# GpSimd scales the softmax probabilities by a scalar per partition instead of a repeated column

## Chip, core and metric

The kernel runs on one core of one Trainium2 chip. The metric is the device time of one execution in microseconds (us). A core has five engines that the text names as the profile does: PE (TensorE, matmuls), PEld (its weight loads), DVE (VectorE), ACT (ScalarE), POOL (GpSimd) and SP (SyncE, which issues most transfers).

## What is computed

A decoder trunk of two layers on 512 tokens plus 16 learned meta tokens in front, width 1024. Each layer has one input projection and two token mixers: a multi-scale causal pooling, and a latent attention with 8 heads. The change lies in the attention's softmax:

```python
s = jnp.einsum('bqhd,bkhd->bhqk', q[:, q0:kend], k[:, :kend]).astype(jnp.float32) * scale
s = jnp.where(valid, s, MASK_VALUE)
p = jax.nn.softmax(s, axis=-1).astype(v.dtype)
outs.append(jnp.einsum('bhqk,bkhd->bqhd', p, v[:, :kend]))
```

Everything around it is matrix products with the layer's weights:

```python
proj = h @ w_in[l]
y_pool = (pool_mix(u_pool, pool_w_group[l], pool_scale[l]) * jax.nn.silu(z_pool)) @ pool_w_up[l]
y_mla = (o_mla * jax.nn.silu(z_mla)) @ mla_w_up[l]
merged = jax.nn.sigmoid(g_pool) * y_pool + jax.nn.sigmoid(g_mla) * y_mla
h_res = h_res + merged @ w_out[l]
```

## The kernel before

Activations stand with channels on the 128 partitions and the 528 tokens along the free axis. Nearly every product is made in three matmuls (`mm3`, lines 188, 191 and 192): weight and activation are each split into a high and a low part, and high x high, high x low and low x high are summed. A weight chunk of 128x512 is fetched by SP (`raw`), its high part is made by ACT (line 183, `whi`) and its low part by DVE (line 184, `wlo`, which reads `raw` and `whi`). `stream()` goes through all these products in a fixed plan and loads three chunks ahead.

The heads of attention are woven into this stream: `go` calls `prep`, `head` and `pv` head by head, and `gap` fills the time between them with stream work. `prep` makes a head's keys: DVE scales one half (line 847) and POOL the other (line 848). `head` makes the scores of four blocks of 128 queries in PSUM, masks them and takes the row extreme on DVE (line 877), makes the exponentials with their row sums on ACT (line 884) and the reciprocals of the sums, `rs`, on DVE (line 917). The exponentials of the four blocks stand in `pt`: block 0 and 1 in one tile `pa` (144 and 272 columns), block 2 in `pb` (400) and block 3 in `pc` (528), the last two in slots that the profile calls `cq`. The 128 queries of a block are its partitions, so `rs[:, i:i+1]` is one number per partition. POOL then scales each block by it: the 16 columns of the meta tokens go into `pm` (line 922, two heads side by side), the rest is scaled in place (line 924). That makes eight POOL instructions per head, one after the other, for 16 heads.

`pv` reads the result for the head before: PE transposes the scaled tiles (line 944), ACT and DVE split them (`split`, lines 295 and 296), and PE multiplies them with the values (lines 949 and 950). In every second head ACT and DVE also split `pm` (lines 937 to 939) for a small product of its own (line 955). ACT's line 964 and DVE's line 965 empty the one PSUM bank `o`. In the second layer, `mixed`, `fast` and `got_gp` add combinations of activations on DVE between the heads, for a product of the gates that needs seven block products instead of eight.

Instructions are written out in Python order, but the order on each engine is set by a scheduler when the kernel is built (`schedule_with_timeline_sim=True`), which places instructions by the durations that it assumes for them. Each engine then runs its own list in that order and waits on semaphores.

Of the kernel before, what the change touches and what calls it, by code (L numbers as in the profile page):

```python
# [14 lines left out]
ALU = mybir.AluOpType  # L15
# [3 lines left out]
P = 128  # L19
# [3 lines left out]
NM = 16  # L23
# [49 lines left out]
def trunk(ctx, tc, xT, pos, win, wkr, wqb, wkb, wvb, wgr, wpu, wmu, wout, gains, const, yT):  # L73
    nc = tc.nc
    pe, act, dve, gp, sp = nc.tensor, nc.scalar, nc.vector, nc.gpsimd, nc.sync
# [11 lines left out]
    def nm(s):  # L87
        uid[0] += 1
        return f"{s}_{uid[0]}"

    def slot(tag, dt=F32, bufs=1, w=W):
        return sl.tile([P, w], dt, tag=tag, name=nm(tag), bufs=bufs)
# [10 lines left out]
    def sct():  # L103
        return pp.tile([P, 512], F32, tag="S", name=nm("S"), bufs=3)
# [82 lines left out]
    def mm3(out, wh, wl, xh, xl, start, stop, more=False, hold=False):  # L187
        first = pe.matmul(out, wh, xh, start=start, stop=False, skip_group_check=more)  # L188
        if hold:
            behind(first, newest[0])  # L190
        pe.matmul(out, wh, xl, start=False, stop=False, skip_group_check=more)  # L191
        newest[0] = pe.matmul(out, wl, xh, start=False, stop=stop, skip_group_check=more)  # L192
        past.append((clk[0], newest[0]))
# [163 lines left out]
    class Layer:  # L357
# [503 lines left out]
        def head(self, h, kq, prev, between):  # L861
            kh, kl, qh, ql = kq
            odd = h % 2
            nqs, hold = self.nqs, h == 0
            pa = slot("pa", bufs=2, w=416)
            pb = slot(f"cq{8 + odd}")
            pc = slot(f"cq{10 + odd}")
            bia = sm.tile([P, 5], F32, tag="bia", name=nm("bia"), bufs=2)
            rs = sm.tile([P, 5], F32, tag="rs", name=nm("rs"), bufs=2)

            def scores(i, out, a, b):
                q0 = NM + P * i
                mm3(out, qh[:, q0:q0 + P], ql[:, q0:q0 + P], kh[:, a:b], kl[:, a:b], True, True,
                    hold=hold and i == 1)

            def top(i, c, sv, mask):
                dve.tensor_tensor_reduce(out=sv, in0=sv, in1=mask, scale=nqs[:, i, h:h + 1], scalar=3e38,  # L877
                                         op0=ALU.add, op1=ALU.min, accum_out=bia[:, c:c + 1])

            def causal(n):  # L880
                return maskw[:, 512 - n:]

            def expo(i, c, sv, pv):
                act.activation(pv, sv, AF.Exp, scale=-1.0, bias=bia[:, i:i + 1], accum_out=rs[:, c:c + 1])

            pt = [pa[:, 0:144], pa[:, 144:416], pb[:, 0:400], pc[:, 0:T]]
            sa = sct()
            s1, s3 = sa[:, 0:272], sa[:, 272:272 + SPL]
            scores(1, s1, 0, 272)
            scores(3, s3, 0, SPL)  # L890
            top(1, 1, s1, causal(272))
            top(3, 4, s3, maskw[:, 0:SPL])
            sb = sct()
            s2 = sb[:, 0:400]
            scores(2, s2, 0, 400)
            if not self.last:
                mm3(sb[0:NM, 400:416], qh[:, 0:NM], ql[:, 0:NM], kh[:, 0:NM], kl[:, 0:NM], True, True)
                dve.tensor_add(self.smeta[:, h, :], sb[0:NM, 400:416], cst[0:NM, C_MM:C_MM + NM])
            top(2, 2, s2, causal(400))
            expo(1, 1, s1, pt[1])  # L900
            expo(2, 2, s2, pt[2])
            self.gap()
            between()
            self.pv(prev, (0, 1))
            self.gap()
            sc = sct()
            s0, s4 = sc[:, 0:144], sc[:, 144:144 + T - SPL]
            scores(3, s4, SPL, T)
            scores(0, s0, 0, 144)
            top(3, 3, s4, causal(T - SPL))  # L910
            top(0, 0, s0, causal(144))
            dve.tensor_tensor(out=bia[:, 3:4], in0=bia[:, 3:4], in1=bia[:, 4:5], op=ALU.min)
            expo(3, 4, s3, pt[3][:, 0:SPL])
            expo(3, 3, s4, pt[3][:, SPL:T])
            expo(0, 0, s0, pt[0])
            dve.tensor_add(rs[:, 3:4], rs[:, 3:4], rs[:, 4:5])
            dve.reciprocal(rs[:, 0:4], rs[:, 0:4])  # L917
            if odd == 0:
                self.pm = sm.tile([P, 4, 32], F32, tag="pm", name=nm("pm"), bufs=2)
            for i in range(4):  # L920
                n = pt[i].shape[1]
                gp.tensor_mul(self.pm[:, i, 16 * odd:16 * odd + 16], pt[i][:, 0:NM],  # L922
                              rs[:, i:i + 1].to_broadcast([P, NM]))
                gp.tensor_mul(pt[i][:, NM:], pt[i][:, NM:], rs[:, i:i + 1].to_broadcast([P, n - NM]))  # L924
            return h, pt, self.pm

        def pv(self, prev, js):
# [365 lines left out]
```

## Time and profile before

| | |
|---|---|
| three runs | 788.27, 788.89 and 788.9 us; median 788.89 |
| the profiled execution | 788.28 us, of which the span of the program's instructions is 786.4 us |
| PE, PEld | busy 778.8 and 713.4 us |
| DVE, ACT | busy 558.8 and 427.1 us |
| POOL | busy 210.9 us in 275 instructions |
| PE's granted clock | full speed throughout |
| DMA | 97.6 MB, 124 GB/s on average |

The times in the profile are those of the profiled execution. An engine counts as busy from the start to the end of each of its instructions; PE's ends are modelled. The heads of the first layer lie between about 190 and 335 us of the span, those of the second between about 580 and 720 us.

### The profile page before, as it was taken

Reading aid. Unit: us, or ns where it says so; the run is one execution under the profiler, and the core shown is the slowest. Engines: PE = TensorE matmul, PEld = TensorE weight load, DVE = VectorE, ACT = ScalarE, POOL = GpSimd, SP = SyncE. Lnnn points to the kernel's source line nnn. Section 1 sums busy time; section 2 is a strip of 40 time slices with the busy share of each in tenths; the row PEclk is TensorE's granted clock in tenths of the full one; section 3 lists DMA queues with packets and bytes.
Section 4 is the critical chain, followed back from the end, with each engine's and each line's share of the span. In section 5 each row is a group of like instructions: output and inputs, shape, how many; then the busy total and the mean of one; then the engine's idle time right before and its main releaser. Section 6 shows DMA issues by size and latency. Waiting matters only on the chain.

```text
span 786.4 us, 15094 instructions
## 1 busy us (share of the span) xinstructions
PE 778.8 (99%) x5445; PEld 713.4 (91%) x5445; DVE 558.8 (71%) x1229; ACT 427.1 (54%) x974; POOL 210.9 (27%) x275
## 2 busy tenths in 40 slices
PE   9999999999999999999999999999999999999998
PEld 8999899999999999999997898887778999887887
DVE  5848778447788977685355487775897899874932
ACT  8545655635656665643354455556657676654421
POOL 1034504002434342153000145122004323440600
PEclk9999999999999999999999999999999999999999
DMA  6242343434645435647742422435233454462372
GB/s 243 82 101 84 99 120 102 128 106 117 136 122 126 116 90 112 167 103 176 206 141 81 109 81 79 138 97 167 95 111 112 118 153 126 121 202 68 99 231 100
DMA packets 60907, 97.61 MB, mean 124 GB/s; under 512 B 9744, under 2 KB 18320, under 8 KB 60832
## 3 DMA queue, kind: packets, MB, share of 16 engines
q1 hardware_dynamic: 57520, 90.61, 38.8%
q0 software_dynamic: 2304, 4.20, 4.3%
q10 hardware_dynamic: 1008, 1.84, 0.7%
q8 instruction: 43, 0.70, 0.4%
q14 instruction: 32, 0.26, 0.1%
HBM read 88.64 MB, written 14.23 MB: 131 GB/s over the span
## 4 chain that ended last, share of the span: by engine, by line
PE 91%; DVE 4%; DMA 2%; issue 1%; ACT 1%; ACTq 0%; DVEq 0%
PE mm L188 27%; PE mm L192 27%; PE mm L191 26%; PE mm L944 2%; PE S L191 2%; PE S L192 2%; PE S L188 1%; DVE wlo L184 1%; PE o L950 1%; PE o L949 1%; PE S L498 1%; PE mm L400 1%; DMA xb<-xT 1%; DMA raw<-win 1%; DVE hl L296 0%
## 5 line engine op out<-in xcount | busy, mean ns | idle before, releaser
L188 PE MATMUL mm<-hh,whi 128*128 128x264 f32 (+2 forms) x1080 | 333.9, 311 | 0.1
L191 PE MATMUL mm<-hl,whi 128*128 128x264 f32 (+2 forms) x1080 | 332.5, 309 | 0.4 <-DVE hl L296 0.4
L192 PE MATMUL mm<-hh,wlo 128*128 128x264 f32 (+2 forms) x1080 | 332.1, 310 | 0.4 <-DVE wlo L184 0.4
L184 DVE TENSOR_TENSOR wlo<-raw,whi 128x512 fp32r<-128x512 f32 (+2 forms) x263 | 197.7, 756 | 108.8 <-ACT whi L183 105.3
L183 ACT ACTIVATE whi<-raw 128x512 fp32r<-128x512 f32 (+2 forms) x263 | 157.8, 603 | 179.3 <-PE mm L191 114.6
L188 PEld LDWEIGHTS mm<-hh,whi 128*128 128x128 f32 x1080 | 202.9, 188 | 11.8 <-ACT racc L958 0.5
L191 PEld LDWEIGHTS mm<-hl,whi 128*128 128x128 f32 x1080 | 203.3, 188 | 11.1 <-DVE hl L296 0.9
L192 PEld LDWEIGHTS mm<-hh,wlo 128*128 128x128 f32 x1080 | 202.5, 188 | 10.5 <-DVE wlo L184 1.1
L700 POOL TENSOR_TENSOR racc<-racc,tmp 128x264 f32<-128x264 f32 (+1 forms) x15 | 14.2, 950 | 144.2 <-ACT tmp L699 119.8
L192 PE MATMUL mm<-cq,wlo 128*128 128x264 f32 (+2 forms) x140 | 43.5, 313 | 0.6 <-DVE wlo L184 0.6
L188 PE MATMUL mm<-cq,whi 128*128 128x264 f32 (+2 forms) x140 | 44.0, 314 | 0.0
L191 PE MATMUL mm<-cq,whi 128*128 128x264 f32 (+2 forms) x140 | 43.4, 311 | 0.0
L848 POOL TENSOR_TENSOR tmp<-kp,bc 64x528 f32<-64x528 f32 x16 | 23.7, 1484 | 68.5 <-PE mm L815 44.4
L1049 POOL TENSOR_TENSOR tmp<-tmp,xb 128x264 f32<-128x264 f32 (+1 forms) x24 | 27.2, 1155 | 50.4 <-DVE tmp L1047 38.9
L877 DVE CUSTOM_DVE_ANT_0 S<-S,maskw,nqs 128x288 f32<-128x288 f32 (+4 forms) x80 | 38.3, 497 | 3.0 <-PE S L192 2.8
L922 POOL TENSOR_TENSOR pm<-pa,rs 128x16 f32<-128x16 f32 x32 | 10.9, 340 | 96.7 <-DVE rs L917 88.6
L188 PE MATMUL mm<-u,whi 128*128 128x264 f32 (+1 forms) x108 | 35.2, 326 | 0.1
L296 DVE TENSOR_TENSOR tl<-mm,th 128x512 fp32r<-128x512 f32 (+1 forms) x64 | 29.4, 481 | 7.7 <-ACT th L295 6.5
L192 PE MATMUL mm<-u,wlo 128*128 128x264 f32 (+1 forms) x108 | 34.7, 322 | 0.0
L924 POOL TENSOR_TENSOR cq<-cq,rs 128x384 f32<-128x384 f32 (+1 forms) x32 | 32.8, 1024 | 0.0
L191 PE MATMUL mm<-kn,whi 128*128 128x264 f32 (+1 forms) x96 | 30.6, 320 | 0.0
L188 PE MATMUL mm<-q,whi 128*128 128x264 f32 (+1 forms) x96 | 29.9, 323 | 0.6 <-ACT q L295 0.4
(309 smaller groups left out, 1472.3 us busy)
## 6 DMA issues: line engine op xcount, KB each, us to landing
raw<-win SPq DMA_DIRECT2D x139, 256.0 KB, 2.7
raw<-wout SPq DMA_DIRECT2D x32, 256.0 KB, 3.3
bc<-kdr SPq DMA_DIRECT2D x16, 264.0 KB, 4.1
raw<-wpu SPq DMA_DIRECT2D x16, 256.0 KB, 2.8
wsum<-win SPq DMA_DIRECT2D x16, 256.0 KB, 3.3
raw<-wmu SPq DMA_DIRECT2D x16, 256.0 KB, 2.8
raw<-wsum SPq DMA_DIRECT2D x16, 256.0 KB, 3.2
raw<-wqb SPq DMA_DIRECT2D x12, 256.0 KB, 2.6
```

The lines of the kernel that those rows point to most:

```text
L183: act.activation(hi[:, :n], raw[:, :n], AF.Copy)
L184: dve.tensor_sub(lo[:, :n], raw[:, :n], hi[:, :n].bitcast(F32))
L188: first = pe.matmul(out, wh, xh, start=start, stop=False, skip_group_check=more)
L191: pe.matmul(out, wh, xl, start=False, stop=False, skip_group_check=more)
L192: newest[0] = pe.matmul(out, wl, xh, start=False, stop=stop, skip_group_check=more)
L296: dve.tensor_sub(lo[:, a:b], src, hi[:, a:b].bitcast(F32))
L700: self.acc_last = gp.tensor_add(self.acc[:, a:b], self.acc[:, a:b], t[:, :b - a])
L848: gp.tensor_mul(kf[r0:r0 + 64, :], self.kp[r0:r0 + 64, :], bc[r0:r0 + 64, :])
L877: dve.tensor_tensor_reduce(out=sv, in0=sv, in1=mask, scale=nqs[:, i, h:h + 1], scalar=3e38, op0=ALU.add, op1=ALU.min, accum_out=bia[:, c:c ...
L924: gp.tensor_mul(pt[i][:, NM:], pt[i][:, NM:], rs[:, i:i + 1].to_broadcast([P, n - NM]))
L944: pe.transpose(tr[:, P * (i - j):P * (i - j + 1)], pt[i][:, NM + P * j:NM + P * (j + 1)], ident)
L1049: gp.tensor_add(t[:, :b - a], t[:, :b - a], self.am[m][:, a:b])
```

## The change

Where POOL multiplied a tile by `rs`'s column read again for every element (a second tensor with a step of zero), it now runs the operation that multiplies a tile by one scalar per partition, read from the same place. The values, the tiles and the number of instructions are the same, in both layers.

```diff
             for i in range(4):
-                n = pt[i].shape[1]
-                gp.tensor_mul(self.pm[:, i, 16 * odd:16 * odd + 16], pt[i][:, 0:NM],
-                              rs[:, i:i + 1].to_broadcast([P, NM]))
-                gp.tensor_mul(pt[i][:, NM:], pt[i][:, NM:], rs[:, i:i + 1].to_broadcast([P, n - NM]))
+                gp.tensor_scalar(self.pm[:, i, 16 * odd:16 * odd + 16], pt[i][:, 0:NM], rs[:, i:i + 1], None, op0=ALU.mult)
+                gp.tensor_scalar(pt[i][:, NM:], pt[i][:, NM:], rs[:, i:i + 1], None, op0=ALU.mult)
```

The changed kernel is two lines shorter, so line 944 of before is line 942 of after, and 937 is 935. The scheduler assumes another duration for the new operation, and so the order on PE, DVE, ACT and SP changes too, within the heads of both layers; outside them it is the same.

On PE, in the first head of the first layer, the transposes of the scaled tiles stood together. `pa` holds blocks 0 and 1, `cq_459` block 2 and `cq_460` block 3; `mm_2825` and `mm_2836` are the PSUM banks that they are transposed into. Before and after:

```order
L191 MATMUL mm_2750<-hl_21_143,whi_2746 128x264
L192 MATMUL mm_2750<-hh_20_142,wlo_2747 128x264
L944 MATMUL mm_2825<-cst,pa_2530 128x128 x2
L944 MATMUL mm_2825<-cst,cq_459_2531 128x128
L944 MATMUL mm_2825<-cst,cq_460_2532 128x128
L944 MATMUL mm_2836<-cst,pa_2530 128x128
L944 MATMUL mm_2836<-cst,cq_459_2531 128x128
L944 MATMUL mm_2836<-cst,cq_460_2532 128x128
```

```order
L191 MATMUL mm_2750<-hl_21_143,whi_2746 128x264
L192 MATMUL mm_2750<-hh_20_142,wlo_2747 128x264
L942 MATMUL mm_2825<-cst,pa_2530 128x128 x2
L942 MATMUL mm_2836<-cst,pa_2530 128x128
L188 MATMUL mm_2751<-hh_14_136,whi_2746 128x264
L191 MATMUL mm_2751<-hl_15_137,whi_2746 128x264
L192 MATMUL mm_2751<-hh_14_136,wlo_2747 128x264
L942 MATMUL mm_2825<-cst,cq_459_2531 128x128
L942 MATMUL mm_2836<-cst,cq_459_2531 128x128
```

The transposes of block 2 moved behind three matmuls; those of block 3 come further down, out of this piece.

On PE, in the fourth head of the second layer, `cq_1584_8244` is block 3 and `cq_1583_8243` block 2; `S_8620` are scores of the next head. Before:

```order
L188 MATMUL S_8620<-kh_8425,qhl_105 128x144
L191 MATMUL S_8620<-kl_8426,qhl_105 128x144
L192 MATMUL S_8620<-kh_8425,qhl_106 128x144
L944 MATMUL mm_8549<-cst,cq_1584_8244 128x128
L944 MATMUL mm_8560<-cst,pa_8242 128x128
L944 MATMUL mm_8560<-cst,cq_1583_8243 128x128
L944 MATMUL mm_8560<-cst,cq_1584_8244 128x128
L188 MATMUL mm_8468<-hh_14_136,whi_8579 128x256
```

After, the transposes of block 3 stand here:

```order
L192 MATMUL mm_8530<-sq_7748,wlo_8602 128x256
L188 MATMUL mm_8530<-rinv_7752,whi_8601 128x256
L191 MATMUL mm_8530<-rinv_7752,whi_8601 128x256
L192 MATMUL mm_8530<-rinv_7752,wlo_8602 128x256
L942 MATMUL mm_8549<-cst,cq_1584_8244 128x128
L942 MATMUL mm_8560<-cst,cq_1584_8244 128x128
L953 MATMUL mm_8570<-identr,pmr_8545 96x128 x4
```

They moved from right behind the scores to behind the 12 matmuls into `mm_8468` and the 12 into `mm_8530`.

On ACT, at the same head, the split of `pm` (line 937, now 935). Before:

```order
L183 ACTIVATE whi_8526<-raw_8524 128x512
L623 ACTIVATE sv_8481<-mm_8468 128x256
L937 ACTIVATE pmr_8545<-pm_8119 128x4x32
L964 ACTIVATE tmp_8450<-o_8313 64x512
L884 ACTIVATE cq_1636_8484,rs_8487<-S_8497,bia_8486 128x400
L183 ACTIVATE whi_8579<-raw_8577 128x512
```

After:

```order
L183 ACTIVATE whi_8526<-raw_8524 128x512
L623 ACTIVATE sv_8481<-mm_8468 128x256
L884 ACTIVATE pa_8483,rs_8487<-S_8488,bia_8486 128x272
L183 ACTIVATE whi_8579<-raw_8577 128x512
L962 ACTIVATE tmp_8450<-o_8313 64x512
L183 ACTIVATE whi_8601<-raw_8599 128x512
L935 ACTIVATE pmr_8545<-pm_8119 128x4x32
```

Two weight splits, an exponential and the emptying of `o` now stand ahead of it. On POOL the eight instructions of a head stand as before, with TENSOR_SCALAR in place of TENSOR_TENSOR; one L848 of the first layer moved ahead of a head's eight.

## The prediction

> **What bounds the kernel now.** I read the page's busy line first, then the chain that ended last, then busy time by stretch, and only then GpSimd (POOL).
>
> ```profile
> PE 778.8 (99%) x5445; PEld 713.4 (91%) x5445; DVE 558.8 (71%) x1229; ACT 427.1 (54%) x974; POOL 210.9 (27%) x275
> PE 91%; DVE 4%; DMA 2%; issue 1%; ACT 1%; ACTq 0%; DVEq 0%
> ```
>
> Busy time by stretch: start and end, length, then PE, weight loads, DVE, ACT and POOL, clock, DMA share and GB/s.
>
> ```profile
> 190.00:335.00 145.00, 144.65 (x1175) 142.82 (x1174) 115.41 (x285) 86.95 (x224) 52.63 (x80) 1.00 0.53 124
> 580.00:700.00 120.00, 119.10 (x779) 107.90 (x779) 109.05 (x263) 83.87 (x216) 45.69 (x70) 1.00 0.45 135
> ```
>
> TensorE (PE) is busy 99% of the span and carries 91% of the chain; POOL stands nowhere on it. The two stretches are the attention heads of the two layers, where the edited lines run. PE idles 0.35 us in the first and 0.90 us in the second. So little can be won: whatever POOL saves, PE's work stays. What can be lost depends on who waits for POOL. DVE is the second engine to watch: in the second layer's heads it is busy 109.05 of 120 us, 91%, with 10.95 us idle; in the first layer's it has 29.6 us.
>
> **The change, part by part.** It swaps 128 POOL instructions one for one, eight in each of 16 heads: four that copy 16 scaled columns into pm and four that scale the rest in place. Groups by line and shape (busy us, mean ns):
>
> ```profile
> L924 POOL TENSOR_TENSOR cq<-cq,rs 128x512 f32<-128x512 f32 x16 | 17.2, 1078 | 0.0
> L924 POOL TENSOR_TENSOR cq<-cq,rs 128x384 f32<-128x384 f32 x16 | 15.5, 970 | 0.0
> L924 POOL TENSOR_TENSOR pa<-pa,rs 128x256 f32<-128x256 f32 x16 | 11.4, 711 | 0.0
> L924 POOL TENSOR_TENSOR pa<-pa,rs 128x128 f32<-128x128 f32 x16 | 7.5, 471 | 0.0
> L922 POOL TENSOR_TENSOR pm<-cq,rs 128x16 f32<-128x16 f32 x32 | 13.7, 429 | 0.0
> L922 POOL TENSOR_TENSOR pm<-pa,rs 128x16 f32<-128x16 f32 x32 | 10.9, 340 | 96.7 <-DVE rs L917 88.6 <-DVE tl L296 8.1
> ```
>
> Single lines, with the shortest, median and longest in ns:
>
> ```profile
> L924 POOL TENSOR_TENSOR cq<-cq,rs x32: 822/1036/1682, 191.8 to 697.3; 128x384 f32<-128x384 f32 x16, 128x512 f32<-128x512 f32 x16
> L924 POOL TENSOR_TENSOR pa<-pa,rs x32: 395/609/1104, 189.8 to 694.3; 128x128 f32<-128x128 f32 x16, 128x256 f32<-128x256 f32 x16
> L922 POOL TENSOR_TENSOR pm<-pa,rs x32: 208/218/664, 189.7 to 694.1; 128x16 f32<-128x16 f32 x32
> L773 POOL CAST vb<-tmp x8: 289/292/755, 97.8 to 495.6; 32x128 fp32r<-32x128 f32 x8
> L474 POOL COPY tmp<-tmp x4: 398/778/810, 71.7 to 469.7; 32x264 f32<-32x264 f32 x4
> ```
>
> Undisturbed, the four big ones take 0.40, 0.61, 0.82 and 1.04 us (395, 609, 822, 1036 ns) and each small one 0.21: 1.66 ns an element above a fixed 0.18. The groups' means are longer, which the DVE part explains. No row shows POOL multiplying by a scalar per partition, so I bound it. Below: the operations with one input, 289 ns for 128 elements and 398 for 264, thus 0.80 ns an element; 512 elements would take 0.60 us, 0.6 of now. Above: the longest rows of these same instructions (1682 and 1104 in L924, 664 in L922), about twice the undisturbed ones. An extra scalar to fetch, with two operation slots of which one is empty, argues for longer; one stream fewer argues for shorter. POOL's price follows its program rather than the bytes: a copied element and an element multiplied by one repeated value differ by a factor of two. The nearest row in arithmetic is L924 itself, and I take 1.5 times it, midway to the upper end. That is my weakest choice.
>
> **Readers on PE.** The transposes of L944 read the scaled tiles. The tightest places, both in the second layer, by the timeline (start, length):
>
> ```profile
> 593.81 0.52 POOL L922 TENSOR_TENSOR pm<-pa,rs 128x16 f32<-128x16 f32 x1 [33.96 <-DVE rs L917]
> ...
> 594.82 0.62 POOL L924 TENSOR_TENSOR pa<-pa,rs 128x256 f32<-128x256 f32 x1
> 596.25 0.51 PE L944 MATMUL mm<-cst,pa 128*128 128x128 f32 x3
> ...
> 636.69 0.22 POOL L922 TENSOR_TENSOR pm<-pa,rs 128x16 f32<-128x16 f32 x1 [8.11 <-DVE tl L296]
> 639.56 1.04 POOL L924 TENSOR_TENSOR cq<-cq,rs 128x512 f32<-128x512 f32 x1
> 642.15 0.29 PE L944 MATMUL mm<-cst,cq 128*128 128x128 f32 x1
> 645.32 0.28 PE L192 MATMUL mm<-rinv,wlo 128*128 128x256 f32 x1
> ```
>
> At 636.69 a burst of eight begins and ends at 640.60, after 3.9 us; the last tile is read at 642.15, 1.55 us later. At 1.5 times the burst ends at 642.6, too late for the old place. But the order has moved that read behind 24 matmuls of 256 columns, whose last stood at 645.32: cover of 2.7 us. At 594.82 the second tile ends at 595.44 and is read about 596.4; from 593.81 on it takes 1.6 us, at 1.5 times 2.4, so 596.2: just in time. PE waits for POOL in none of the two: 0. If the price were double, the first burst would end at 644.5 (still covered) and the second tile at 597.1, a wait of 0.7 us.
>
> **ACT.** The split of pm at L937 waits for POOL's small operations, with weight splits (L183) queued behind it. From the waits (us, times, longest):
>
> ```profile
> ACT pmr L937 <- POOL pm L922: 10.4, 7, 3.0
> ```
>
> That is 10.4 us in seven waits. The order puts this split later in seven of eight pairs of heads, so up to two weight splits and other work now pass ahead of it. A burst of 1.5 times ends 2 us later, and what passes ahead covers most of that. ACT has 36 us idle between 580 and 700, so I charge 0; without that cover the eight waits would be longer by up to 2 us each, 16 us on ACT.
>
> **DVE.** This is the term that I charge. POOL and DVE block each other, by the timeline:
>
> ```profile
> 598.10 1.34 POOL L848 TENSOR_TENSOR tmp<-kp,bc 64x528 f32<-64x528 f32 x1
> ...
> 612.86 1.03 POOL L924 TENSOR_TENSOR cq<-cq,rs 128x512 f32<-128x512 f32 x1
> 612.96 1.50 DVE L847 TENSOR_TENSOR tmp<-kn,bc 64x528 f32<-64x528 f32 x1
> 613.85 1.78 POOL L848 TENSOR_TENSOR tmp<-kp,bc 64x528 f32<-64x528 f32 x1
> 614.49 1.70 DVE L184 TENSOR_TENSOR wlo<-raw,whi 128x512 fp32r<-128x512 f32 x1
> ...
> 670.63 0.69 DVE L184 TENSOR_TENSOR wlo<-raw,whi 128x512 fp32r<-128x512 f32 x1
> ```
>
> L847 alone (shortest, median, longest), and the DVE groups between 580 and 700 us:
>
> ```profile
> L847 DVE TENSOR_TENSOR tmp<-kn,bc x16: 673/706/1712, 154.0 to 676.5; 64x528 f32<-64x528 f32 x16
> L184 DVE TENSOR_TENSOR wlo<-raw,whi 128x512 fp32r<-128x512 f32 x46 | 37.3, 812 | 3.5 <-ACT whi L183 3.2
> L847 DVE TENSOR_TENSOR tmp<-kn,bc 64x528 f32<-64x528 f32 x7 | 6.4, 912 | 0.1
> L855 DVE TENSOR_TENSOR qhl<-q,qhl 64x512 fp32r<-64x512 f32 x6 | 4.9, 821 | 0.1
> ```
>
> PE's own waits in the second layer's heads, and the chain around one of them:
>
> ```profile
> PE o L949 <- DVE tmp L965: 0.5, 1, 0.5
> PE mm L188 <- DVE sv L625: 0.3, 1, 0.3
> ```
>
> ```profile
> 614.71 1.48 DVE wlo L184
> 616.19 0.61 DVE tmp L965
> 616.84 0.50 PE o L949
> ```
>
> L847, begun while L924 ran, took 1.50 us against a median of 0.71; L184, begun under L848, took 1.70 against 0.69 when free, and PE's L949 stood behind it and L965 at 616.84. These DVE operations have two inputs in SBUF. [...]
>
> In the second layer's heads the blocking adds up, from the last groups, to 46 x (812 - 690) + 7 x (912 - 706) + 6 x (821 - 690) = 5.6 + 1.4 + 0.8 = 7.8 us. A wait is on average half of what it hits, and longer operations are hit more often, so blocking goes with the square of POOL's durations: per head 4 x 0.21² + 0.40² + 0.61² + 0.82² + 1.04² = 2.46 for the changed ones, 1.34² = 1.80 for L848. The changed ones' share is 58%, 4.5 us. At 1.5 times: 4.5 x (2.25 - 1) = 5.6 us more, half of DVE's idle time there. What of it reaches PE? Today 0.90 us of PE's idle time against 7.8, an eighth, would make it 0.65; all of it would make it 5.6. With the idle time halved I take a third, 1.9 us. The first layer's DVE has 29.6 us to absorb the same: 0.
>
> Nothing else is paid for: the numbers of instructions are the same, and the order differs within the heads alone.
>
> **Sum.** The profiled execution took 788.28 us (span 786.4), so 788.28 + 1.9 = 790.2. That execution is at the low end of the three runs; on their median, 788.89, it is 790.8, which I forecast. Its own range is 789.5 to 794.5, from the 0.65 and the 5.6.
>
> **The rivals.** *Shorter (chance 0.28), not slower.* With one stream at 0.80 ns an element the eight take 0.6 of the time, the squares fall to 1.0 against 2.46, and DVE regains 2.7 us. PE can regain at most its idle time, 0.90 + 0.35 = 1.25 us; half of that gives 788.3. It decides where an element costs less than 1.66 ns. For it speak the one-input rows, against it that they do no arithmetic. [...]
>
> *Same price (0.15).* The scalar is read like the repeated column, and only the moved order counts: 788.9, half a microsecond either way.
>
> *Double (0.20).* Blocking grows by 4.5 x 3 = 13.5 us, 2.6 more than DVE's idle time. That 2.6, a third of the 10.95 and the 0.7 of the late tile make 7: 795.9. It decides from about 1.9 times on, where DVE has no idle time left.
>
> *Three times or more (0.05).* The burst at 636.69 ends at 648.4, 3.1 us behind the read at 645.3, and so in most heads: some 40 us more, 830.
>
> The forecast has 0.32. The range, 787.2 to 797.0, reaches from the shorter rival's bound (788.89 - 1.25, less the runs' spread) past the double one, and leaves out the last. About 0.2%, 1.6 us, is what a measurement of this kernel can tell from no change. Faster by more: 0.07 of the shorter rival, whose gain would have to come from PE time that the modelled ends hide, 0.02 of the same price, 0.01 of the forecast: 0.10. Slower by more: 0.18 of the forecast, 0.20, 0.05, and 0.05 of the others for a moved order that goes wrong: 0.48. Between: 0.42.
>
> **What would show it.** In the new profile, the scaling rows: 1.5 us for 512 elements is my case, 0.6 the shorter rival, 2.1 the double. Then DVE's L184 in the second layer's heads: a mean above 812 ns with my case, below it with the shorter one. PE's waits should name DVE there, not POOL. I am wrong in mechanism if PE or PE's chain waits for the scaled tiles themselves, or if time is lost in the first layer's heads; wrong in size if the rows leave 0.6 to 2 times.

## The result and the profile after

The changed kernel takes 792.88 us (792.25 to 794.11, four runs) against 788.65 us (788.27 to 788.90) for the kernel before on the same chip: a ratio of 1.0056, with a 95% interval of 1.0039 to 1.0073. It is slower by 4.2 us by the medians, 4.4 by the ratio. The profiled execution took 792.93 us, with a span of 791.2 us.

The busy line and the chain that ended last, of the changed kernel's page:

```profile
PE 780.7 (99%) x5445; PEld 713.6 (90%) x5445; DVE 553.4 (70%) x1229; ACT 427.2 (54%) x974; POOL 242.0 (31%) x275
...
PE 88%; DVE 5%; issue 2%; ACT 2%; POOL 2%; DMA 1%; POOLq 0%; DVEq 0%; ACTq 0%
```

POOL is busy 31.1 us longer and now stands on the chain. DVE is busy 5.4 us less, although its instructions are the same. Busy time in the heads of the two layers (stretch, length, then PE, weight loads, DVE, ACT and POOL):

```profile
190.00:335.00 145.00, 144.38 (x1171) 142.09 (x1171) 110.98 (x282) 86.13 (x222) 67.35 (x81) 1.00 0.51 123
...
580.00:700.00 120.00, 116.62 (x760) 104.58 (x760) 102.48 (x251) 79.22 (x202) 55.41 (x62) 1.00 0.45 132
```

PE idles 0.62 us in the first layer's heads (0.35 before) and 3.38 us in the second layer's (0.90 before). The loss sits in the second. Row against row (each matmul beside the one of the same number in PE's list of the other trace) PE falls 4.3 us further behind the kernel before between 577 and 723 us. Idle time understates this: over the whole span it grows by 2.9 us, and PE's busy time, whose ends are modelled, by 1.9 for the same 5445 instructions. The scaling operations, single lines with shortest, median and longest in ns:

```profile
L922 POOL TENSOR_SCALAR pa<-pa,rs x32: 592/920/1686, 190.2 to 705.1; 128x128 f32<-128x128 f32 x16, 128x256 f32<-128x256 f32 x16
L922 POOL TENSOR_SCALAR cq<-cq,rs x32: 1236/1558/1762, 193.0 to 708.3; 128x384 f32<-128x384 f32 x16, 128x512 f32<-128x512 f32 x16
L921 POOL TENSOR_SCALAR pm<-cq,rs x32: 317/324/860, 192.7 to 708.0; 128x16 f32<-128x16 f32 x32
```

The shortest rows are 592 for 395, 1236 for 822 and 317 for 208 ns: 1.5 times the old price at every size. The DVE groups between 580 and 700 us, and what PE waited for in the whole run:

```profile
L184 DVE TENSOR_TENSOR wlo<-raw,whi 128x512 fp32r<-128x512 f32 x44 | 32.8, 745 | 6.0 <-ACT whi L183 5.5
L847 DVE TENSOR_TENSOR tmp<-kn,bc 64x528 f32<-64x528 f32 x7 | 5.9, 845 | 0.1
L855 DVE TENSOR_TENSOR qhl<-q,qhl 64x512 fp32r<-64x512 f32 x6 | 4.4, 732 | 0.1
```

```profile
PE mm L188 <- DVE sv L625: 1.1, 2, 0.6
PE S L188 <- ACT kh L295: 1.1, 2, 0.6
...
PE mm L942 <- POOL pa L922: 0.3, 1, 0.3
```

All three DVE groups have become shorter (812, 912 and 821 ns before), where the prediction had them longer. New among PE's waits are the scores (S) that wait for ACT's split of the scaled keys, kh, and one wait for a scaled tile.

### The profile page after: what moved, and what is told of

It reads as the page before. It is cut to its first block, busy times and chain, and to the rows that moved or that the text cites. A ratio compares the mean times of both kernels' runs of the same rounds, so it can differ in the third digit from the quotient of the medians.

```text
span 791.2 us, 15106 instructions
## 1 busy us (share of the span) xinstructions
PE 780.7 (99%) x5445; PEld 713.6 (90%) x5445; DVE 553.4 (70%) x1229; ACT 427.2 (54%) x974; POOL 242.0 (31%) x275
## 3 DMA queue, kind: packets, MB, share of 16 engines
q10 hardware_dynamic: 1008, 1.84, 0.7%
## 4 chain that ended last, share of the span: by engine, by line
PE 88%; DVE 5%; issue 2%; ACT 2%; POOL 2%; DMA 1%; POOLq 0%; DVEq 0%; ACTq 0%
PE mm L188 26%; PE mm L192 26%; PE mm L191 26%; PE mm L942 2%; DVE wlo L184 1%; PE S L191 1%; PE S L192 1%; PE S L188 1%; PE o L948 1%; PE o L947 1%; PE S L498 1%; ACT whi L183 1%; DMA xb<-xT 1%; PE mm L400 1%; POOL pm L921 1%
## 5 line engine op out<-in xcount | busy, mean ns | idle before, releaser
L184 DVE TENSOR_TENSOR wlo<-raw,whi 128x512 fp32r<-128x512 f32 (+2 forms) x263 | 195.5, 746 | 109.1 <-ACT whi L183 104.5
L192 PEld LDWEIGHTS mm<-hh,wlo 128*128 128x128 f32 x1080 | 202.6, 188 | 10.4 <-DVE wlo L184 0.9
L921 POOL TENSOR_SCALAR pm<-pa,rs 128x16 f32<-128x16 f32 x32 | 18.5, 578 | 101.9 <-DVE rs L917 90.0
L922 POOL TENSOR_SCALAR cq<-cq,rs 128x384 f32<-128x384 f32 (+1 forms) x32 | 46.4, 1451 | 0.0
L848 POOL TENSOR_TENSOR tmp<-kp,bc 64x528 f32<-64x528 f32 x16 | 22.4, 1400 | 62.0 <-PE mm L815 44.4
L884 ACT ACTIVATE cq<-S,bia 128x400 f32<-128x400 f32 (+2 forms) x48 | 24.5, 513 | 11.2 <-DVE bia L912 7.7
```

The source lines that it names most:

```text
L184: dve.tensor_sub(lo[:, :n], raw[:, :n], hi[:, :n].bitcast(F32))
L848: gp.tensor_mul(kf[r0:r0 + 64, :], self.kp[r0:r0 + 64, :], bc[r0:r0 + 64, :])
L921: gp.tensor_scalar(self.pm[:, i, 16 * odd:16 * odd + 16], pt[i][:, 0:NM], rs[:, i:i + 1], None, op0=ALU.mult)
L922: gp.tensor_scalar(pt[i][:, NM:], pt[i][:, NM:], rs[:, i:i + 1], None, op0=ALU.mult)
```

## Experiments

The change does two things: it makes POOL's operations longer, and the planner (the scheduler that sets the order when the kernel is built) sets another order. Seven of the kernels part the two by fixing the order. At the end of the trace each engine's instructions are chained in a given order, which is taken from one of the two kernels:

```
+    for row in ORDER:                      # one row for each engine, instruction numbers
+        last = None
+        for n in row:
+            if last is not None:
+                tc.add_manual_dep(made[n], last, DependencyInfo(DependencyClass.NoSync, DependencyReason.DATA))
+            last = made[n].name
```

This adds no wait, only order. One kind of instruction is not held by it: VectorE's 80 operations that mask the scores and take the row extreme (line 877), which the planner still places. Against the kernel whose order they take, 24 of them stand one to four places earlier in the price alone, 6 are off by one place in the order alone and in the last two runs of this section, and none in the two controls. All other instructions of PE, DVE, ACT and POOL stand in the given order in these kernels. Line numbers in these runs are two higher than in the kernel whose code they hold.

**What the fixing costs.** The kernel before in its own order, and the changed one in its own.

> The kernel before with every engine's instructions fixed in the order that they have anyway: what the fixing itself costs, on which the runs with the order alone and the price alone rest. Nothing is expected of it by either theory: a ratio of 0.999 to 1.001. Were it 1.002 or more, the costs read from those runs would be too high by as much.

> The changed kernel once more, fixed in its own order, beside the control on the same chip: 1.0056 as in the first comparison if the fixing costs nothing (1.0040 to 1.0075).

Measured: 788.84 us, ratio 1.0002 (0.9993 to 1.0011), and 792.94 us, 1.0055 (1.0038 to 1.0072). The fixing costs nothing, and the changed kernel's loss comes out again.

**Order alone, price alone.** The old operations in the changed kernel's order, and the new operations in the order of before.

> The old multiplication (the tensor that repeats a column) with every engine's instructions fixed in the order that they have in the changed kernel, so only the order differs from the kernel before. Theory 1, the longer operations cost the time directly: the order alone is worth nothing, 788.4 to 789.2 us. Theory 2, the planner's new order costs most of it and the longer operations the rest (from the stalls in the changed kernel's trace: 0.46 us where TensorE waits for a scaled tile and 0.81 us where the key scaling stands behind a longer burst, about 1.3 us together; 3 us left): 791 to 792 us. [...]

> The scaling by a scalar per partition, as changed, with every engine's instructions fixed in the order of the kernel before, so only the price differs. Theory 1 (price): 792 to 794 us, since the order of before places the readers of the scaled tiles earlier than the changed one does, with TensorE waiting at the first blocks' transposes. Theory 2 (order): 789.5 to 790.5 us. Both: GpSimd's 512-column operations last 1.56 us and VectorE's L184 between 580 and 700 us has a mean below the 812 ns of before, as in the changed kernel.

Measured: the order alone 791.03 us, 1.0041 (1.0028 to 1.0055); the price alone 802.32 us, 1.0187 (1.0173 to 1.0201). The first lies in theory 2's range: 3.2 us by the ratio, 3.5 by the medians. The second is what neither theory expected: 14.8 us, more than three times the whole change. So the parts do not add. Left in the old order the longer operations cost 14.8 us; in the planner's new order the whole change costs 4.4 us, and that order costs 3.2 us with the old operations. How much the 24 operations of VectorE that moved in the price alone add to its 14.8 us was not parted.

Where the price goes is in the trace of the price alone. It is paid in both layers: row against row PE falls 6.2 us behind in the first layer's heads and 6.7 in the second's. The first layer's:

```profile
190.00:335.00 145.00, 142.02 (x1130) 138.77 (x1129) 106.11 (x270) 82.43 (x216) 68.24 (x81) 0.99 0.47 116
```

Not all of it is waiting. PE's granted clock, which is 1.00 in the heads of the two kernels, was 0.50 here from 234.25 to 237.66 us, right behind a stall of 1.93 us at 233.02, and that is about 1.7 us more. All four times of this run come with a mean clock below full: 801.54 and 801.58 us at 0.998, 803.07 and 803.66 at 0.996. That the stall brought the clock down is not shown; no drop follows the longer stall below.

POOL, ACT and PE around the longest stall (start, length; in brackets the idle time before and what ended it):

```profile
624.28 1.56 POOL L924 TENSOR_SCALAR cq<-cq,rs 128x512 f32<-128x512 f32 x1
625.81 1.28 POOL L850 TENSOR_TENSOR tmp<-kp,bc 64x528 f32<-64x528 f32 x1
627.13 0.64 ACT L297 ACTIVATE kh<-tmp 128x528 fp32r<-128x528 f32 x1 [3.69 <-POOL tmp L850]
627.82 0.70 PE L190 MATMUL S<-kh,qhl 128*128 128x272 f32 x3 [2.62 <-ACT kh L297]
```

L850 (L848 in the two kernels) scales the next head's keys. It is not part of the change, but it stands on POOL right behind a burst of eight scalings, and ACT's kh and PE's scores wait for it in turn: PE sits idle for 2.62 us. The same chain in the waits, first of the kernel before and then of the price alone (us, times, longest), with ACT's wait for the 16-column tiles:

```profile
ACT kh L295 <- POOL tmp L848: 3.6, 4, 2.0
```

```profile
ACT pmr L937 <- POOL pm L923: 21.7, 8, 4.4
...
ACT kh L297 <- POOL tmp L850: 14.7, 6, 4.0
```

ACT's wait for the scaled keys grows from 3.6 to 14.7 us. DVE's weight split in the second layer's heads, of the price alone (busy us, mean ns):

```profile
L186 DVE TENSOR_TENSOR wlo<-raw,whi 128x512 fp32r<-128x512 f32 x41 | 29.8, 726 | 5.0 <-ACT whi L185 4.6
```

Against 812 ns before, with the weight splits in the same order: the longer operations keep DVE out for less. DVE's busy time says so too: 558.8 us in the kernel before and in the order alone, 548.9 in the price alone.

**The key scaling ahead of the burst.** The price alone once more, with one kind of instruction moved on POOL in four heads: in the first layer's fourth head and the second layer's third, fourth and seventh.

```
 POOL, order of before
+L848 tmp<-kp,bc 64x528
 L922 pm<-pa,rs 128x16
 ... seven more scalings
-L848 tmp<-kp,bc 64x528
```

> The run with the price alone (the changed scaling in the order of the kernel before, 802.3 us), with one thing altered on GpSimd's queue: in four of the heads the next head's key scaling stands ahead of the burst of eight behind which it stood. Nothing else moves. Theory 1, the longer bursts cost their time through the key scaling that queues behind them (in the trace of the price alone ScalarE's kh split starts 0.03 us after the key scaling ends, at 232.3, 608.9, 627.1 and 687.3 us, and TensorE's scores behind it lose 2.1 us and some 1.7 us after it, then 2.9 and 1.3 us): about 8 us come back, 793.5 to 796.5 us. Theory 2, they cost it through the scaled tiles themselves, which come late to TensorE's transposes and now 1.3 us later still in four heads: 802 to 807 us.

Measured: 793.87 us, 1.0063 (1.0042 to 1.0084). With four instructions moved, 8.4 us come back by the medians (9.8 by the ratios), as theory 1 said, though the scaled tiles behind them are ready 1.3 us later. Some of it is clock: here the mean granted clock is 1.0 in all four runs. ACT's wait is down from 14.7 us:

```profile
ACT kh L297 <- POOL tmp L850: 3.3, 2, 2.4
```

That the loss goes through the queue behind the burst, more than through the scaled tiles, is shown by this run and by these waits. It isn't quite as clean as its plan: 10 of VectorE's 80 mask operations, which the fixing does not hold, moved with it by one to three places.

**One layer at a time.** The diff is applied under a condition on the layer; the planner is free.

```
+                if self.l == 0:        # e5: == 1
                     gp.tensor_scalar(...)
+                else:
+                    gp.tensor_mul(..., rs[:, i:i + 1].to_broadcast(...))
```

> The change in the first layer alone; the second layer keeps the multiplication by a repeated column. The planner gives the first layer's heads the order of the changed kernel and the second layer's the order of the kernel before. Theory 1, the loss is in the second layer's heads, as the traces place it (the changed kernel is 0.4 us behind from 335 to 592 us): a ratio of 1.000 to 1.001 to the kernel before, 788.4 to 789.2 us where that takes 788.6. Theory 2, the loss sits in both layers as the work does: half of 4.2 us, ratio 1.0027.

> The change in the second layer alone; the planner gives the first layer's heads the order of before and the second layer's that of the changed kernel. Theory 1: the whole loss less 0.4 us, a ratio of 1.0045 to 1.0055 to the kernel before. Theory 2: half of it, 1.0027.

Measured: the first layer alone 1.0002 (0.9992 to 1.0013), the second alone 1.0053 (1.0032 to 1.0073). With the planner free, all that can be measured lies in the second layer. In the old order the first layer pays as well, as the price alone shows.

**Prices by themselves.** A kernel that does nothing but these operations, executed once.

> GpSimd's operations measured by themselves, and VectorE's subtraction of two 128x512 SBUF tiles beside them; nothing of the model is computed. Four of each size alone: the scaling by a scalar per partition 317, 592, 917, 1237 and 1558 ns for 16, 128, 256, 384 and 512 columns, the multiplication by the repeated column 210, 397, 609, 822 and 1036 ns, as in the two traces; the multiplication by a full second tensor is not in these traces. Then 36 subtractions of VectorE alone (693 ns each) and beside 24 operations of 512 columns. Theory A (that of the prediction), a GpSimd operation keeps VectorE out for its whole length whatever its form: beside the scalar form a subtraction lasts longer than beside the repeated column, towards 1.56 + 0.69 = 2.25 us against 1.04 + 0.69 = 1.73 us. Theory B, the scalar form keeps VectorE out only for its first third (0.54 of 1.56 us): 24 operations cost the subtractions beside them about 24 x 0.54 = 13 us, against 25 us beside the repeated column, where VectorE and GpSimd take turns.

Groups by line and shape while POOL works alone (L120 scalar, L124 a full second tensor, L116 the repeated column):

```profile
L120 POOL TENSOR_SCALAR g<-g,rs 128x512 f32<-128x512 f32 x4 | 6.2, 1562 | 0.0
L124 POOL TENSOR_TENSOR g<-g,full 128x512 f32<-128x512 f32 x4 | 4.9, 1262 | 0.0
L116 POOL TENSOR_TENSOR g<-g,rs 128x512 f32<-128x512 f32 x4 | 4.0, 1038 | 0.0
L120 POOL TENSOR_SCALAR g<-g,rs 128x256 f32<-128x256 f32 x4 | 3.6, 922 | 0.0
L124 POOL TENSOR_TENSOR g<-g,full 128x256 f32<-128x256 f32 x4 | 2.8, 722 | 0.0
L116 POOL TENSOR_TENSOR g<-g,rs 128x256 f32<-128x256 f32 x4 | 2.3, 612 | 0.0
```

Between 256 and 512 columns an element costs 2.50 ns with the scalar, 2.11 with a full second tensor and 1.66 with the repeated column. Then with DVE's subtractions beside them, the same columns, first beside the repeated column and then beside the scalar:

```profile
L127 DVE TENSOR_TENSOR part<-a,b 128x512 f32<-128x512 f32 x25 | 34.7, 1387 | 0.8
L116 POOL TENSOR_TENSOR g<-g,rs 128x512 f32<-128x512 f32 x24 | 34.3, 1463 | 0.0
```

```profile
L120 POOL TENSOR_SCALAR g<-g,rs 128x512 f32<-128x512 f32 x18 | 33.0, 1853 | 0.0
L127 DVE TENSOR_TENSOR part<-a,b 128x512 f32<-128x512 f32 x35 | 30.4, 869 | 1.2
```

Beside the repeated column the two take turns: one subtraction to each POOL operation, 1.39 us long on average (1.41 row by row once both run) where it takes 0.69 free. Beside the scalar two subtractions pass to each POOL operation, and the row by row view has them in turn at 692 and 1061 ns: 0.37 us lost to an operation of 1.84 us. So a scalar operation costs DVE half of what a repeated-column one costs (0.72 us), though it is 1.5 times as long. Theory A falls. Theory B's direction holds, with 0.37 us in place of the 0.54 that I expected; that this is the operation's first third is not shown.

**Wide tiles first.** The four 128-column-and-wider scalings of a head ahead of the four of 16 columns, with the old operation and with the new, planned anew.

```
             for i in range(4):
-                <scale 16 columns into pm>
                 <scale the rest of pt[i] in place>
+            for i in range(4):
+                <scale 16 columns into pm>
```

> The old multiplication, with the four wide tiles of a head scaled first and the four operations of 16 columns last; the same eight operations, planned anew. Every wide tile is ready 0.2 to 0.8 us earlier and the burst ends when it did. Theory 1, a new plan is neutral when the prices are the same, and only waits on the bursts cost time: a ratio of 0.999 to 1.001 to the kernel before. Theory 2, any new plan of the second layer's heads moves the time by as much as the changed kernel's order did by itself (3.2 us): a ratio off 1 by 0.002 to 0.005, either way.

> The scaling by a scalar per partition, with the four wide tiles first and the four operations of 16 columns last, planned anew. Every wide tile is ready 0.3 to 1.3 us earlier than in the changed kernel and the burst ends when it did. If the loss came through the scaled tiles, most of it goes: a ratio to before of 1.000 to 1.002. If it comes through the key scaling behind the burst and through the order that the planner makes of it, it stays: 1.004 to 1.008.

Measured: the old operation 790.29 us, 1.0021 (1.0009 to 1.0033); the new one 795.66 us, 1.0089 (1.0065 to 1.0113). With the new operation this gains nothing: 1.0089, above both ranges that I had stated, stands against the changed kernel's 1.0056. With the old one, a new plan of the same eight operations costs about 1.7 us, as theory 2 had it. How much of either is the 16-column tiles' later place and how much the plan was not parted.

**What the order costs, at one place.** In the order alone, the split of the third head's keys in the second layer, put back to where before has it.

```
 ACT, order of after                          DVE, order of after
+L295 kh<-tmp 128x528                        +L296 kl<-tmp,kh 128x528
 L884 three exponentials                      L916 rs<-rs, L917 rs<-rs
 L183 whi<-raw 128x512 x2                     L184 wlo<-raw,whi 128x512 x2
-L295 kh<-tmp 128x528                        -L296 kl<-tmp,kh 128x528
```

> The run with the order alone (old multiplication in the changed kernel's order, ratio 1.0041), with one pair of instructions put back: in the second layer's third head the split of the scaled keys stands where the kernel before has it, ScalarE's kh ahead of the three exponentials of the second half and VectorE's kl ahead of the row sums, and not behind two more weight splits on each engine. Theory 1, the order costs by such places, where the planner puts the key split back for a key scaling that it expects late: the two stalls of TensorE at this head's scores (0.88 us at 603.7 and 0.99 us at 605.3 us of the run with the order alone) go, 1.5 to 1.9 us come back, a ratio of 1.0017 to 1.0022. Theory 2, the stalls only move on to the next late operand (the weight splits that now come behind): 1.0035 to 1.0045.

The place in the order alone, by the timeline of POOL, ACT and PE:

```profile
598.23 1.34 POOL L850 TENSOR_TENSOR tmp<-kp,bc 64x528 f32<-64x528 f32 x1
602.01 1.15 ACT L185 ACTIVATE whi<-raw 128x512 fp32r<-128x512 f32 x2
603.05 0.64 ACT L297 ACTIVATE kh<-tmp 128x528 fp32r<-128x528 f32 x1
603.75 0.71 PE L190 MATMUL S<-kh,qhl 128*128 128x272 f32 x3 [0.63 <-ACT kh L297]
605.31 0.39 PE L193 MATMUL S<-kl,qhl 128*128 128x272 f32 x1 [0.74 <-DVE kl L298]
```

and, from the kernel before, the split at its old place:

```profile
599.93 0.63 ACT L295 ACTIVATE kh<-tmp 128x528 fp32r<-128x528 f32 x1
```

The key scaling ends at 599.57 in the order alone, but kh starts only at 603.05, behind three exponentials and two weight splits; before, it starts 0.49 us after its keys. With the longer burst the key scaling ends at 602.4 us (601.05 and 1.35 in the changed kernel's trace), and the later place fits better: PE idles 0.42 us for kh there and not at all for kl, against 0.63 and 0.74. In the run with the split put back:

```profile
601.71 0.65 ACT L297 ACTIVATE kh<-tmp 128x528 fp32r<-128x528 f32 x1 [0.67 <-POOL tmp L850]
604.97 0.68 PE L190 MATMUL S<-kh,qhl 128*128 128x272 f32 x3
605.89 0.37 PE L193 MATMUL S<-kl,qhl 128*128 128x272 f32 x1
```

The two stalls are gone: row against row PE regains 0.88 and 0.94 us there and loses 0.32 between them to another operand (ACT's tc), 1.5 us in all. The time is 790.90 us, 1.0032 (1.0019 to 1.0044), between what the two theories expected; by times alone the run is inconclusive. About 1.5 us of the order's 3.2 come from this place by this trace. The rest is open. The trace of the order alone names small waits of the same kind (DVE's L977 and ACT's racc, late for PE), which I did not undo.

**What the price costs in the new order.** The changed kernel in its own order, with the seventh head's key scaling in the second layer ahead of the burst. Its place in the changed kernel:

```profile
675.82 1.56 POOL L922 TENSOR_SCALAR cq<-cq,rs 128x512 f32<-128x512 f32 x1
677.47 1.50 POOL L848 TENSOR_TENSOR tmp<-kp,bc 64x528 f32<-64x528 f32 x1
679.00 0.64 ACT L295 ACTIVATE kh<-tmp 128x528 fp32r<-128x528 f32 x1 [1.94 <-POOL tmp L848]
679.70 0.70 PE L188 MATMUL S<-kh,qhl 128*128 128x272 f32 x3 [0.65 <-ACT kh L295]
```

> The changed kernel in its own order, but for one instruction on GpSimd's queue: in the second layer the key scaling at 677.5 us stands ahead of the burst of eight (669.2 to 677.4 us) behind which it stood. Theory 1, what the longer operations still cost in the new order is mainly this one place: TensorE's 0.81 us at 679.7 us and most of the 0.8 us behind it go, the burst's own readers lose nothing, a ratio to before of 1.0035 to 1.0045 (the changed kernel: 1.0056). Theory 2, the scaled tiles that come 1.5 us later cost as much again: 1.0055 to 1.0075.

Measured: 790.94 us, 1.0033 (1.0020 to 1.0046). With this one instruction moved:

```profile
677.33 0.63 ACT L297 ACTIVATE kh<-tmp 128x528 fp32r<-128x528 f32 x1
679.59 0.69 PE L190 MATMUL S<-kh,qhl 128*128 128x272 f32 x3
```

and its busy time in the second layer's heads:

```profile
580.00:700.00 120.00, 117.55 (x768) 105.92 (x767) 104.22 (x258) 81.41 (x210) 55.09 (x62) 1.00 0.45 135
```

PE's idle time in the second layer's heads falls from 3.38 to 2.45 us. Row against row it regains 0.89 us at these scores and 1.5 us in the next 10 us, and gives 0.55 back at 698 us. The moved burst's readers lose nothing. The time is close to theory 1's range, and its interval leaves out theory 2's; but it overlaps the changed kernel's, so the times do not show the gain by themselves.

The rows do. PE's list is the same in the changed kernel, in the order alone and in this run. Between 577 and 723 us PE falls 4.3, 2.6 and 2.3 us behind the kernel before. From 619 to 675 us the changed kernel is no further behind than the order alone (within 0.02 us); what differs before cancels. The 1.8 us between them arise behind this one key scaling. The 0.89 us at the scores are its alone; for the rest, 6 of VectorE's mask operations that stand one place off there may have a part.

No run beat the kernel before. PE idles only 1.25 us there in the heads of both layers together, so there is little that this line of work could win.

## Why the prediction was right, and where it was not

The measured 792.88 us lies inside the range and on the side forecast, 2.1 us above the 790.8. That it came so near is luck: the one term that was charged has the wrong sign, and two paths that were not charged stand in its place.

- **The price** was right to the figure: 1.5 times at every size. The choice between the bounds, named as the weakest, held. The shorter rival's 0.80 ns an element, taken from rows with one input, does not hold for a scalar per partition: by themselves an element costs 2.50 ns with the scalar, 2.11 with a full second tensor and 1.66 with the repeated column. Why the scalar form is the longest is not shown; the extra scalar and the two operation slots were my argument for it, not a measurement.
- **Readers on PE, 0**: nearly right. The tile called just in time, due at 596.2, made PE wait, 0.46 us at 597.19 row against row (0.28 us of idle time). The one at 636.69 was covered by the moved order, as worked out; in the old order PE loses 0.95 us there.
- **ACT's split of pm, 0**: right. The new order cut that wait from 10.4 to 7.4 us; without it the price alone shows 21.7 us, 11 more where I had bounded 16.
- **DVE, +1.9 us**: the step that failed. I let a POOL operation keep DVE out for its whole length, so that blocking grows with the square of the durations. That was an estimate from single rows of before, and no run shows the square or the term. By themselves, beside the repeated column (1.04 us long when alone), the two engines take turns: a pair takes 1.445 us, where one after the other would be 1.73, and a subtraction loses 0.72 us. Beside the scalar, 1.5 times as long at 1.56 us, DVE loses half as much, 0.37 us. DVE's three groups became shorter, and its busy time fell by 5.4 us. The term's sign was wrong.
- **"Nothing else is paid for", the order at 0**: the term that was missing. The order costs 3.2 us and the price in that order the remaining 1.2 or so (2.6 and 1.8 by PE's rows). I read the order only for the readers of the scaled tiles and asked there whether it covers them. It moved the split of the keys as well, by 3 us in the second layer's third head.
- **What POOL's queue holds behind the burst**: missed, though my own rows showed it. They have L924 at 612.86 for 1.03 us and L848 at 613.85, right behind it. One more row, kh released by L848, would have named the path PE depends on. In the old order this path was worth 8 to 10 of 14.8 us, the slower clock behind one of its stalls included.
- **First layer, 0**: right, 1.0002, but not because DVE has time there: in the price alone PE falls 6.2 us behind in that layer's heads, and only the new order avoids it.
- **The signs named beforehand**: L184 below 812 ns spoke against my case at once, and PE's chain now shows POOL. The DVE mechanism was wrong by its own test.

## What to carry to other kernels

When an operation becomes longer on an engine that works through its list in order, as POOL does in these traces, look first at what is queued right behind it on that engine and who waits for that, and only then at its own readers: here an untouched key scaling behind the burst cost more than the scaled tiles did. Where a planner sets the order, a changed price is also a changed order; run each alone, with the order fixed, before crediting either with the difference, since the two need not add up (14.8 and 3.2 us gave 4.4). Here the new order cost 3.2 us even with the fast operations. And check what a fixed order leaves free: here it was one kind of VectorE's instructions.

## What the hardware showed that I had not expected

- On GpSimd working alone, a multiplication by a scalar per partition took 0.28 us and 2.50 ns for each element of a row (922 ns for 256, 1562 for 512), more than one by a full second tensor (2.11 ns) and half as much again as one by a column repeated with a step of zero (1.66 ns).
- How long these GpSimd operations kept VectorE out did not follow their length. Beside 512 columns with the repeated column, a subtraction of VectorE lost 0.72 us (0.69 to 1.41) and the POOL operation 0.44 (1.04 to 1.48). With the scalar the losses were 0.37 us on VectorE, once for every two subtractions, and 0.28 on POOL (1.56 to 1.84). In the changed kernel three groups of VectorE's operations with both inputs in SBUF became shorter in the second layer's heads: L184 took 745 ns on average (812 before), L847 845 (912) and L855 732 (821). Over the whole run its splits that read PSUM (`tl`) stayed within 2% (684 for 687 ns at 512 columns, 281 for 276 at 128), and so did the split of the keys, `kl`, with both inputs in SBUF (698 for 704).
- PE's granted clock fell in the middle of a kernel: in the trace of the price alone it was 0.50 for 3.4 us, behind a stall of 1.93 us. In the heads of the changed kernel, where no stall of PE reaches 0.7 us, it stayed at 1.00.
